# The rests of the MLP weights: added up by transfers from GpSimd's queue instead of subtracted on VectorE

## The chip, the cores and the metric

The kernel runs on one core of one Trainium2 chip. The metric is the device time of one execution in microseconds, lower is better; it is given as the median of the runs shown. The profile comes from one further execution, taken by the hardware profiler; its times are its own.

## The reference

The model is a two-layer decoder trunk for 512 tokens of width 1024, all in float32. Each layer mixes tokens by two kinds of attention, adds the result to the residual `x`, and then runs a squared-ReLU MLP. The change touches only the MLP:

```python
h = rmsnorm(x, norm_mlp)
return x + jnp.square(jax.nn.relu(h @ w_up)) @ w_down      # w_up: 1024 x 4096, w_down: 4096 x 1024
```

## The kernel before, in words

**Two-part numbers.** TensorE multiplies in a rounded 32-bit format. To keep float32's accuracy the kernel splits each operand into a rounded part `h` and a rest `lo` = operand minus `h`, and makes each product of three: `h·xh`, `h·xl` and `lo·xh` (lines 212 to 214 in `gemm`, line 1196 in `Strassen.product`). A product thus needs the rest only in its third step. The rests of weights have to be made on the chip, because the weights arrive as plain float32.

**Loaded weight tiles.** `plan` lists the weight tiles in the order of their use. `fetch` (line 164) issues the load of the next one from SyncE into a tile called `raw`, of 128x1024 numbers. `convert` (line 173) takes the oldest loaded tile, makes `wh` by a cast on ScalarE (line 186) and `wl` by a subtraction on VectorE (line 187), and then calls `fetch` for the next. `ahead`, called from inside `gemm`, converts one tile in advance. `wh` and `wl` have two buffers each.

**The MLP.** `mlp` first computes 8 of the 32 column blocks of `h @ w_up` plainly. The other 24 go through `Strassen`: twelve units, g4 to g15, each of two column blocks, made of seven products of half the size (`unit`, line 1204). Each product has 12 multiplications of 256 columns. While unit g runs, the generator `convert(g + 1)` (line 1168) makes the seven operands of the next unit: some are quarters of the loaded `w_up` tiles, some are sums of them. Two of the sums, `s1` and `s3`, are made on GpSimd (lines 1177 and 1178), the others, `s2` and `s4`, on VectorE. Each operand becomes a pair `sh` (cast on ScalarE, line 1186) and `sl` (subtraction on VectorE, line 1187). `sh` and `sl` have eight buffers each. The loads of `w_up` for unit g + 2 are issued at the start of unit g (line 1158), into two pairs of buffers that take turns.

Between the products of a unit, `unit` runs a few down products: chunks of `relu² @ w_down` over the column blocks that are done (`down`). Their weights come through `convert` of the loaded tiles; each tile serves two down products. The units have 2, 2, 3, 3, 4, 4, 4, 4, 4, 4, 2 and 0 of them. Twelve more run before the first unit. The activations that feed them get their rests on GpSimd (`act`, line 1263).

**Order and buffers.** Each engine works through its own instructions in order; a scheduler has merged the parts of the program into these orders when the kernel was built. Tiles come from pools by tag, with a fixed number of buffers (line 153), and a new user of a buffer waits for the last reader of the old one. From its seventh tile on, `w_down` is loaded into tag `crs` (line 703), which has one buffer. The Strassen sums `s` share tag `t2` with the eight residual tiles. No transfer is issued from GpSimd.

Of the kernel before, what the change touches and what calls it, by code (L numbers as in the profile page):

```python
# [11 lines left out]
F32 = mybir.dt.float32  # L12
F32R = mybir.dt.float32r
AF = mybir.ActivationFunctionType
OP = mybir.AluOpType
# [122 lines left out]
def run(*gens):  # L138
    for g in gens:
        for _ in g:  # L140
            pass


class Body:
# [28 lines left out]
    def convert(self):  # L173

        nc = self.nc
        if not self.loaded:
            self.fetch()
        if not self.loaded:
            return
        raw, src, n = self.loaded.popleft()  # L180
        if self.spots:
            h, lo = self.spots.popleft()
        else:
            h = self.t("wh", [128, 1024], F32R)
            lo = self.t("wl", [128, 1024], F32R)
        nc.scalar.copy(h[:, :n], raw[:, :n])  # L186
        nc.vector.tensor_tensor(lo[:, :n], raw[:, :n], h[:, :n].bitcast(F32), op=OP.subtract)  # L187
        self.split.append((h, lo, src, n))
        self.fetch()

# [10 lines left out]
            self.convert()  # L201

    spots = ()
    raws = deque()

    def gemm(self, ps, w, k0, xs, ks=8, start=True, stop=True):
# [705 lines left out]
    def mlp(self, l, x, u, acc, gm):  # L912

        nc, a = self.nc, self.a
        R = None
        pend = []
        acts = []

        def act(ps):
            t = self.t("tmp", [128, T])  # L920
            nc.vector.scalar_tensor_tensor(t, ps, 0.0, R, op0=OP.max, op1=OP.mult)
            h = self.t("oh", [128, T], F32R)
            lo = self.t("ol", [128, T], F32R)
            nc.scalar.activation(t, t, AF.Square)
            nc.scalar.copy(h, t)
            nc.vector.tensor_tensor(lo, t, h.bitcast(F32), op=OP.subtract)
            acts.append((h, lo))

        def down(c, m, w):

            ps = self.bank()
            yield from self.gemm(ps, w, 4 * (m % 2), acts[4 * c:4 * c + 4], ks=4)
            nc.vector.tensor_add(x[m], x[m], ps)

        def downs():
            for c in range(6):
                for m in range(8):
                    if m % 2 == 0:
                        w = self.weights(a["wd2"][l, c, m // 2])
                    yield lambda: run(down(c, m, w))  # L940

        S = Strassen(self, l, x, gm)
        D = downs()
        raws = [None] * 16
        g0 = self.PLAIN // 2
        S.load(g0)
        for j in range(self.PLAIN):
            ps = self.bank()
            w = self.weights(a["wup"][l, j].rearrange("p k c -> p (k c)"))
            run(self.gemm(ps, w, 0, u))  # L950
            if R is None and j == 0:
                pend.append(ps)
                continue
            if R is None:
                R, _ = self.rstd(acc, (self.turn_tag(), self.turn_tag()))
                prep = S.prepare(R)
                for p in pend:
                    act(p)
            act(ps)
            for _ in range(3):  # L960
                next(prep, None)
        conv = S.convert(g0)
        for i in range(12):
            next(D)()
            if i < 7:
                next(prep, None)
                next(prep, None)
            elif i == 7:
                run(prep)
            else:  # L970
                next(conv, None)
                next(conv, None)
            if i == 10:
                S.load(g0 + 1)
        run(conv)
        for g, n in zip(range(g0, 16), (2, 2, 3, 3, 4, 4, 4, 4, 4, 4, 2, 0)):
            S.load(g + 2)
            S.unit(g, D, n, acts)
        u_next = []
        acts = acts[24:]  # L980
        if l + 1 < L:
            acc = []
            self.load_small(l + 1)
            for m in range(8):
                ps = self.bank()
                w = self.weights(a["wdn"][l, m].rearrange("p k c -> p (k c)"))
                run(self.gemm(ps, w, 0, acts))
                nc.vector.tensor_add(x[m], x[m], ps)
                acc = self.sumsq(x[m], acc, m == 7)
                u_next.append(self.make_u(x[m], self.gain[:, 16 * l + 16:16 * l + 24], m))  # L990
                nc.scalar.dma_start(self.xs[m], x[m])
        else:
            self.last(x, acts, a["wdn"][l])
        self.acc = acc
        return u_next
# [105 lines left out]
class Strassen:  # L1101
# [66 lines left out]
    def convert(self, g):  # L1168

        if g == 16:  # L1170
            return
        b, nc = self.b, self.nc
        r1, r2 = self.raw.pop(g)
        a11, a12, a21, a22 = r1[:, :512], r1[:, 512:], r2[:, :512], r2[:, 512:]
        s1, s2, s3, s4 = (b.t("t2", [128, 512], name="s") for _ in range(4))
        G = nc.gpsimd
        G.tensor_tensor(s1, a21, a22, op=OP.add)
        G.tensor_tensor(s3, a11, a21, op=OP.add)
        ops = self.ops[g] = []
        for i, src in enumerate((a11, s1, s2, a22, s3, a12, s4)):  # L1180
            if i == 2:
                nc.vector.tensor_tensor(s2, s1, a11, op=OP.add)
                nc.vector.tensor_tensor(s4, s2, a12, op=OP.add)
            h = b.t("uh", [128, 512], F32R, name="sh")
            lo = b.t("ul", [128, 512], F32R, name="sl")
            nc.scalar.copy(h, src)  # L1186
            nc.vector.tensor_tensor(lo, src, h.bitcast(F32), op=OP.subtract)  # L1187
            ops.append((h, lo))
            yield

# [110 lines left out]
```

## Time and profile before

| | us |
|---|---|
| median of three runs | 1553.21 (1552.73 to 1553.71) |
| the profiled execution | 1552.95 |
| its span, first to last instruction | 1551.2 |
| TensorE busy in the span | 1536.4 (99%) |
| VectorE | 1075.2 (69%) |
| ScalarE | 776.0 (50%) |
| GpSimd | 205.2 (13%) |

PE is TensorE's multiplications, PEld its weight loads, which overlap them; DVE is VectorE, ACT ScalarE, POOL GpSimd, SPq the queue of SyncE that issues most transfers. In rows of groups the columns are the line, engine, operation, the tile written and those read with their shapes and the count; then the busy time in us and the mean of one in ns; then the engine's idle time just before these instructions and what ended it. Rows of a timeline give start and length in us.

### The profile page before, as it was taken

Reading aid. Unit: us, or ns where it says so; the run is one execution under the profiler, and the core shown is the slowest. Engines: PE = TensorE matmul, PEld = TensorE weight load, DVE = VectorE, ACT = ScalarE, POOL = GpSimd, SP = SyncE. Lnnn points to the kernel's source line nnn. Section 1 sums busy time; section 2 is a strip of 40 time slices with the busy share of each in tenths; the row PEclk is TensorE's granted clock in tenths of the full one; section 3 lists DMA queues with packets and bytes.
Section 4 is the critical chain, followed back from the end, with each engine's and each line's share of the span. In section 5 each row is a group of like instructions: output and inputs, shape, how many; then the busy total and the mean of one; then the engine's idle time right before and its main releaser. Section 6 shows DMA issues by size and latency. Waiting matters only on the chain.

```text
span 1551.2 us, 22739 instructions
## 1 busy us (share of the span) xinstructions
PE 1536.4 (99%) x8460; PEld 1306.6 (84%) x8460; DVE 1075.2 (69%) x2204; ACT 776.0 (50%) x1455; POOL 205.2 (13%) x177
## 2 busy tenths in 40 slices
PE   9999999999999999999999999999999999999997
PEld 8877888888888999999887688888888889999997
DVE  5687988766569776664646789887664887766643
ACT  6444655553454555444433456555434635545553
POOL 4000000000201232221400000000002013222222
PEclk9999999999999999999999999999999999999999
DMA  7545422133333322321535543221433333323131
GB/s 240 172 128 154 127 82 82 55 114 117 96 95 123 109 96 95 109 82 64 176 117 165 157 140 100 68 82 55 150 95 95 95 120 99 113 91 99 65 96 55
DMA packets 56638, 169.57 MB, mean 109 GB/s; under 512 B 7344, under 2 KB 8112, under 8 KB 56528
## 3 DMA queue, kind: packets, MB, share of 16 engines
q1 hardware_dynamic: 53072, 161.84, 33.5%
q10 hardware_dynamic: 3456, 6.29, 1.2%
q8 instruction: 66, 1.08, 0.3%
q14 instruction: 44, 0.36, 0.1%
HBM read 140.77 MB, written 4.19 MB: 93 GB/s over the span
## 4 chain that ended last, share of the span: by engine, by line
PE 95%; DVE 3%; ACT 1%; issue 1%; POOL 0%; DMA 0%; DVEq 0%; SPq 0%; POOLq 0%; ACTq 0%
PE ps_mm L212 12%; PE ps_mm L213 12%; PE ps_mm L214 12%; PE ps_S L1196 4%; PE ps_O L1196 4%; PE ps_O L447 4%; PE ps_mm L1196 3%; PE ps_PT L421 3%; PE ps_PT L1196 3%; PE ps_S L212 3%; PE ps_S L213 3%; PE ps_S L214 3%; PE ps_PT L212 3%; PE ps_PT L213 3%; PE ps_PT L214 3%; PE ps_O L212 3%
## 5 line engine op out<-in xcount | busy, mean ns | idle before, releaser
L186 ACT CAST wh<-raw 128x1024 fp32r<-128x1024 f32 (+2 forms) x187 | 192.6, 1030 | 263.7 <-issue 58.5
L187 DVE TENSOR_TENSOR wl<-raw,wh 128x1024 fp32r<-128x1024 f32 (+2 forms) x187 | 226.6, 1212 | 49.8 <-ACT wh L186 48.9
L212 PE MATMUL ps_mm<-uh,wh 128*128 128x512 f32 x512 | 205.1, 401 | 0.0
L214 PE MATMUL ps_mm<-uh,wl 128*128 128x512 f32 x512 | 202.3, 395 | 0.0
L213 PE MATMUL ps_mm<-ul,wh 128*128 128x512 f32 x512 | 202.1, 395 | 0.0
L399 ACT ACTIVATE E<-E,mx 128x128 f32<-128x128 f32 x192 | 108.0, 563 | 82.7 <-DVE mx L398 75.6
L430 ACT CAST pth<-ps_PT 128x512 fp32r<-128x512 f32 x144 | 73.0, 512 | 94.7 <-PE ps_PT L421 94.4
L212 PEld LDWEIGHTS ps_mm<-uh,wh 128*128 128x128 f32 x512 | 96.2, 188 | 26.5 <-issue 10.6
L214 PEld LDWEIGHTS ps_mm<-uh,wl 128*128 128x128 f32 x512 | 96.2, 188 | 20.4 <-issue 0.8
L213 PE MATMUL ps_mm<-ol,wh 128*128 128x512 f32 (+1 forms) x288 | 111.5, 387 | 1.5 <-POOL ol L1263 1.5
L212 PE MATMUL ps_mm<-oh,wh 128*128 128x512 f32 (+1 forms) x288 | 111.8, 388 | 0.0
L214 PE MATMUL ps_mm<-oh,wl 128*128 128x512 f32 (+1 forms) x288 | 111.2, 386 | 0.0
L398 DVE CUSTOM_DVE_ANT_0 E<-ps_S,ct 128x128 f32<-128x128 f32 x192 | 92.2, 483 | 26.5 <-PE ps_S L395 25.0
L213 PEld LDWEIGHTS ps_mm<-ul,wh 128*128 128x128 f32 x512 | 96.4, 188 | 15.1
L431 DVE TENSOR_TENSOR ptl<-ps_PT,pth 128x512 fp32r<-128x512 f32 x144 | 85.0, 595 | 27.6 <-ACT pth L430 27.2
L1187 DVE TENSOR_TENSOR sl<-s,sh 128x512 fp32r<-128x512 f32 x96 | 76.6, 801 | 36.6 <-ACT sh L1186 36.3
L1263 POOL TENSOR_TENSOR ol<-c,oh 128x512 fp32r<-128x512 f32 x48 | 62.7, 1306 | 295.9 <-ACT oh L1262 268.3
L1186 ACT CAST sh<-raw 128x512 fp32r<-128x512 f32 x72 | 44.7, 620 | 106.3 <-PE ps_S L1196 48.1
L1186 ACT CAST sh<-s 128x512 fp32r<-128x512 f32 x96 | 59.3, 620 | 56.4 <-PE ps_PT L1196 19.3
L253 POOL TENSOR_TENSOR acc<-sq 128x512 f32<-128x512 f32 (+1 forms) x6 | 8.4, 1394 | 595.0 <-DVE wl L187 580.1
L421 PE MATMUL ps_PT<-ct,E 128*128 128x128 f32 x480 | 82.9, 273 | 1.4 <-DVE ptl L431 1.4
L421 PEld LDWEIGHTS ps_PT<-ct,E 128*128 128x128 f32 x480 | 60.1, 140 | 14.8 <-DVE ptl L431 4.2
(441 smaller groups left out, 4068.0 us busy)
## 6 DMA issues: line engine op xcount, KB each, us to landing
raw<-wb SPq DMA_DIRECT2D x64, 512.0 KB, 3.2
raw<-wup SPq DMA_DIRECT2D x64, 512.0 KB, 3.7
raw<-wd SPq DMA_DIRECT2D x48, 512.0 KB, 3.5
kd<-hl SPq DMA_DIRECT2D x48, 256.0 KB, 4.6
w<-w SPq DMA_DIRECT2D x32, 256.0 KB, 5.8
q<-hl SPq DMA_DIRECT2D x64, 128.0 KB, 3.2
raw<-wo SPq DMA_DIRECT2D x16, 512.0 KB
raw<-wout SPq DMA_DIRECT2D x16, 512.0 KB, 3.6
```

The source lines that it names most:

```text
L186: nc.scalar.copy(h[:, :n], raw[:, :n])
L187: nc.vector.tensor_tensor(lo[:, :n], raw[:, :n], h[:, :n].bitcast(F32), op=OP.subtract)
L212: mm(ps, h[:, c], xh, start=start and i == 0, stop=False)
L213: mm(ps, h[:, c], xl, start=False, stop=False)
L214: mm(ps, lo[:, c], xh, start=False, stop=stop and i == ks - 1)
L398: nc.vector.tensor_tensor_reduce(e, ps[:, :n], self.mask[:, T - n:], -1.0, BIG, OP.add, OP.min, mx)
L399: nc.scalar.activation(e, e, AF.Exp, bias=mx, scale=-1.0, accum_out=sm[:, i:i + 1])
L421: nc.tensor.transpose(ps[:, j * 128:(j + 1) * 128], E[i][:, b * 128:(b + 1) * 128], self.ident)
L431: nc.vector.tensor_sub(lo[:, o:o + n], ps[:, :n], h[:, o:o + n].bitcast(F32))
L1186: nc.scalar.copy(h, src)
L1187: nc.vector.tensor_tensor(lo, src, h.bitcast(F32), op=OP.subtract)
L1196: self.nc.tensor.matmul(ps, w, x, skip_group_check=True, **kw)
```

## The change

`convert` and `Strassen.convert` no longer subtract on VectorE. Instead ScalarE writes the negative of the rounded part into `lo`, and a transfer issued from GpSimd adds the loaded weight (or the sum) onto it: `lo` = -`h` + operand. For the Strassen operands this holds everywhere; for loaded tiles only while the units run (`by_dma`), which covers 18 tiles of `w_down` in each layer. The casts to `h`, the buffers and the order of the calls stay as they are.

```diff
         nc.scalar.copy(h[:, :n], raw[:, :n])
-        nc.vector.tensor_tensor(lo[:, :n], raw[:, :n], h[:, :n].bitcast(F32), op=OP.subtract)
+        if self.by_dma:
+            self.rest_by_dma(h[:, :n], lo[:, :n], raw[:, :n])
+        else:
+            nc.vector.tensor_tensor(lo[:, :n], raw[:, :n], h[:, :n].bitcast(F32), op=OP.subtract)
         self.split.append((h, lo, src, n))
         self.fetch()
...
+    by_dma = False
+
+    def rest_by_dma(self, h, lo, x):
+
+        self.nc.scalar.activation(lo, h.bitcast(F32), AF.Copy, scale=-1.0)
+        self.nc.gpsimd.dma_start(lo, x, accum_op=OP.add)
...
         run(conv)
+        self.by_dma = True
         for g, n in zip(range(g0, 16), (2, 2, 3, 3, 4, 4, 4, 4, 4, 4, 2, 0)):
             S.load(g + 2)
             S.unit(g, D, n, acts)
+        self.by_dma = False
...
             nc.scalar.copy(h, src)
-            nc.vector.tensor_tensor(lo, src, h.bitcast(F32), op=OP.subtract)
+            b.rest_by_dma(h, lo, src)
             ops.append((h, lo))
```

## The prediction

> **What bounds the kernel now.** I read the page first (busy shares), then the table by stage over the two MLP stretches, then TensorE's waits, and last the chain and the timelines of one MLP unit.
>
> ```profile
> span 1551.2 us, 22739 instructions
> ...
> PE 1536.4 (99%) x8460; PEld 1306.6 (84%) x8460; DVE 1075.2 (69%) x2204; ACT 776.0 (50%) x1455; POOL 205.2 (13%) x177
> ```
>
> ```profile
> 507.00:538.00 31.00, 31.00 (x216) 28.94 (x215) 23.17 (x34) 15.61 (x27) 8.48 (x6) 1.00 0.35 107
> ```
>
> ```profile
> 507.00:726.50 219.50, 218.97 (x1432) 200.66 (x1431) 142.88 (x212) 112.17 (x185) 56.18 (x42) 1.00 0.29 97
> 575.00:701.00 126.00, 126.00 (x795) 114.35 (x795) 82.44 (x121) 64.90 (x106) 31.74 (x25) 1.00 0.28 93
> 1272.00:1480.00 208.00, 207.62 (x1338) 189.49 (x1338) 137.41 (x203) 106.27 (x174) 53.59 (x40) 1.00 0.29 94
> ```
>
> The columns after the stretch and its length are busy us of PE, PEld, DVE, ACT and POOL, then the granted clock, the DMA share and GB/s. Where the change works (units g4 to g15: 507 to 726.5 in the first layer, from 1272 in the second) TensorE stands still for 219.50 - 218.97 = 0.53 us and 208.00 - 207.62 = 0.38 us. VectorE, from which the work is taken, is busy 65% there and nobody on the path waits for it:
>
> ```profile
> PE ps_mm L213 <- POOL ol L1263: 1.5, 2, 1.1
> ...
> PE ps_PT L213 <- POOL ol L1263: 0.4, 1, 0.4
> ```
>
> These are TensorE's only waits in the MLP (us, times, longest), and both are for GpSimd. So there is nearly nothing to win: all of TensorE's idle time in both stretches is 0.9 us, 0.06% of the time. The question is only whether the new way of making the rests stays hidden.
>
> **The unit's clock.** In the chain that ended last, one unit with four down products repeats exactly:
>
> ```profile
> 1346.16 1.43 PE ps_S L1196 x12
> 1347.59 1.44 PE ps_PT L1196 x12
> ...
> 1364.92 0.23 PE ps_mm L214
> ...
> 1367.20 1.43 PE ps_S L1196 x12
> ```
>
> Start, length, instruction. The same product comes again after 1367.20 - 1346.16 = 21.04 us. Seven Strassen products of 1.44 are 10.1, so a down product is (21.04 - 10.1)/4 = 2.74 us. Units with two downs take 15.5 us and with three 18.3. A loaded tile of w_down serves two downs, so in 4-down units one tile is used up every 10.52 us.
>
> **What the change removes and adds.**
>
> ```profile
> L187 DVE TENSOR_TENSOR wl<-raw,wh 128x1024 fp32r<-128x1024 f32 x177 | 218.6, 1235 | 42.2 <-ACT wh L186 41.3 <-DMA raw<-wb 0.5 <-DMA q<-hl 0.2
> ...
> L186 ACT CAST wh<-raw 128x1024 fp32r<-128x1024 f32 x177 | 186.0, 1051 | 249.0 <-issue 58.5 <-PE ps_mm L213 51.2 <-PE ps_O L213 42.6
> ...
> L1187 DVE TENSOR_TENSOR sl<-s,sh 128x512 fp32r<-128x512 f32 x96 | 76.6, 801 | 36.6 <-ACT sh L1186 36.3
> L1263 POOL TENSOR_TENSOR ol<-c,oh 128x512 fp32r<-128x512 f32 x48 | 62.7, 1306 | 295.9 <-ACT oh L1262 268.3 <-DMA raw<-wd 9.2 <-PE ps_S L213 9.2
> ...
> L1186 ACT CAST sh<-s 128x512 fp32r<-128x512 f32 x96 | 59.3, 620 | 56.4 <-PE ps_PT L1196 19.3 <-PE ps_mm L1196 19.3 <-DVE s L1182 7.0
> ...
> L1187 DVE TENSOR_TENSOR sl<-raw,sh 128x512 fp32r<-128x512 f32 x72 | 53.2, 738 | 7.6 <-ACT sh L1186 3.4
> ```
>
> VectorE loses 96 + 72 = 168 subtractions on Strassen operands (76.6 + 53.2 = 130 us) and, by the changed program's instruction list, 36 on w_down tiles (18 a layer, 36 x 1.235 = 44 us). This relief is worth nothing, since no wait of TensorE in these stretches ends on VectorE. ScalarE gains as many negations, priced as the casts of the same shape: 168 x 0.620 + 36 x 1.051 = 142 us. Its tightest place is the two 2-down units: 15.61 busy in 31, plus 14 x 0.62 + 2 x 1.05 = 10.8, gives 26.4 of 31: hidden, if closely. GpSimd gains 204 transfers, which the trace does not show at all: nothing is issued from there before. A 4-down unit gets 7 + 2 = 9 of them. GpSimd is busy 31.74 in 126, so 5.3 in 21.04, which leaves 1.75 us for each issue. The nearest rows for an issue are GpSimd's own operations (1.306): 9 x 1.3 + 5.3 = 17 of 21.04, hidden.
>
> The seven Strassen rests have a whole unit from their cast to their use (21.04 us; 15.5 at least). Cast, negation, issue and transfer are 0.62 + 0.62 + 1.3 and a landing of some 5: hidden. What they do not pass unharmed is GpSimd's queue. In the instruction list the unit's first sum (L1177) stands behind three of the transfers and waits until the second has landed; the w_down transfer stands behind that sum, in the same queue.
>
> **The place where it is tight** is the loaded w_down tile. Its load goes to tag crs, of which there is one buffer, so the next load starts only when the last reader of the tile is done. That reader was VectorE; it becomes the transfer's landing.
>
> ```profile
> 1353.92 0.33 SPq L170 DMA_DIRECT2D raw<-wd  x1
> ...
> 1363.76 0.33 SPq L170 DMA_DIRECT2D raw<-wd  x1
> ```
>
> ```profile
> 1351.59 1.05 ACT L186 CAST wh<-raw 128x1024 fp32r<-128x1024 f32 x1 [1.97 <-PE ps_O L213]
> ...
> 1361.39 1.05 ACT L186 CAST wh<-raw 128x1024 fp32r<-128x1024 f32 x1
> ...
> 1372.63 1.05 ACT L186 CAST wh<-raw 128x1024 fp32r<-128x1024 f32 x1 [1.97 <-PE ps_O L213]
> ```
>
> ```profile
> 1352.67 1.22 DVE L187 TENSOR_TENSOR wl<-raw,wh 128x1024 fp32r<-128x1024 f32 x1 [0.17 <-ACT wh L186]
> ```
>
> ```profile
> raw<-wd SPq DMA_DIRECT2D x48, 512.0 KB, 3.5
> ```
>
> Cast at 1351.59, rest done at 1353.89, next load issued at 1353.92, landed 3.5 later at 1357.4, next cast at 1361.39. The loop has 4.0 us of slack here and 1372.63 - 1363.76 - 3.5 = 5.4 in the next turn, 4.7 in the mean. After the change the loop is cast 1.05, negation 1.05, X (from the negation's end to the transfer's landing), 0.1 for the release, load 3.5: 5.7 + X against 10.52. **It stays hidden up to X = 4.8 us.** Beyond that each tile comes later than the one before by X - 4.8. A first reserve absorbs this: from the cast at 1351.59 to the first product with the rest of that tile (1364.92) are 13.3 us.
>
> **X, from both sides.** Below: the issue at a GpSimd operation's 1.3, and a landing like that of the load of the same 512 KB, 3.5: X = 4.8. (Lower still if the issue is short: 3.5.) Above: this transfer must also read the destination it adds to, so its data time is at least that of two copies, and possibly of more.
>
> ```profile
> q1 hardware_dynamic: 53072, 161.84, 33.5%
> ```
>
> 161.84 MB took 33.5% of 16 engines' 1551.2 us, which is 3.21 us per MB on all 16, so 0.84 us for a 128x512 operand (0.262 MB) and 1.68 for a w_down tile. Twice the data adds 1.7 us, and half of a GpSimd operation standing ahead 0.65: X = 1.3 + 0.65 + 3.5 + 1.7 = 7.15. If the adding took four times a copy, X would be 10.5. I take 7.15: the second read is certain, what goes beyond is not.
>
> A rule speaks for this price: the Trainium skill, "Collectives: The Full Stack", section "The bandwidth ceiling: the fold count and why AG ≠ RS ≠ AR", says that a reduce in the DMA engines reads two sources and so runs at half the copy's rate. No transfer of the trace before shows it; by a plain copy's price X would be 5.5 with the same queueing.
>
> **Sum.** The loop is 5.7 + 7.15 = 12.85, 2.33 over 10.52. Six 4-down units use 12 tiles a layer: 12 x 2.33 = 28, less the reserve 13.3 - (1.05 + 1.05 + 7.15) = 4.0: 24. The DMA engines set a bound of their own: in 4-down units the share 0.28 is 5.9 us, and doubled copies add 2 x (7 x 0.84 + 2 x 1.68) = 18.5, 24.4 in all; this is below the loop's 2 x 12.85 = 25.7, so the loop decides. In the 3-down units it is 0.29 x 18.3 + 2 x (7 x 0.84 + 1.5 x 1.68) = 22.1, 3.8 over; in the 2-down units 0.35 x 15.5 + 2 x (7 x 0.84 + 1.68) = 20.6, 5.1 over. Two of each give 17.8, of which the Strassen operands' reserve of about a unit less its chain (15.5 - 7) absorbs 8.6: 9. A layer loses 24 + 9 = 33 us, both 66. The profiled execution took 1552.95 (span 1551.2 and 1.75 around it; 0.26 under the median 1553.21): 1552.95 + 66 = 1619, so **1620 us, 4.3% slower**.
>
> **Rivals.**
> - *Not slower (0.13).* X stays at or under 4.8. For it speaks that 1.3 + 3.5 is exactly that; against it the second read and the queue in front. It decides at X = 4.8. The time is 1552 to 1555: at best the 0.9 us of idle time go. The Trainium skill, "DMA: Bandwidth & Descriptors", section "Anatomy of one DMA", would give this one: about 2.0 us plus the bytes at 436 GB/s is an estimate of 3.2 us for the tile. No run so far shows such a transfer.
> - *GpSimd becomes the bound (0.15).* If an issue takes two GpSimd operations, 2.6 us, a 4-down unit needs 9 x 2.6 + 5.3 = 28.7, 7.7 over; a 3-down unit 8.5 x 2.6 + 5.3 = 27.4, 9.1 over; a 2-down unit 8 x 2.6 + 4.2 = 25.0, 9.5 over. 12 x 7.7 + 4 x 9.1 + 4 x 9.5 - 17 = 150: 1703 us. It starts at 1.75 us an issue. For it speaks that each carries 128 rows with three accesses; nothing in the trace prices that.
> - *The adding itself is slow (0.12).* At four copies the DMA engines need 5.9 + 37 = 42.9 in a 4-down unit, 21.9 over; with 21 over in the others 12 x 21.9 + 8 x 21 = 430: 1980 us.
>
> **How the numbers follow.** The forecast (DMA landing in the tile's loop, 1575 to 1680) has 0.60, the rivals 0.13, 0.15 and 0.12. About 0.2%, 3.1 us, is what a measurement of this kernel can tell from no change. Faster by more has 0.02: the MLP stretches hold only 0.9 us. Within 0.2% has 0.11, slower 0.87. The range reaches from the hidden case to beyond the GpSimd case, 1553 to 1780; the slow adding is left out above.
>
> **What would show it.** In the changed profile: TensorE waiting in the MLP at the third product of a down triple (the one with wl) for a transfer, about 2 us per tile after the first; loads of w_down 12.8 us apart in 4-down units in place of 9.8 and 11.2; VectorE 174 us less busy, ScalarE 142 more; a DMA share near 0.9 there against 0.28. If GpSimd's sequencer issues without pause, its rival holds. If the transfers land within 4.8 us of the negation's end, there is no loss. The prediction is wrong in size if the landing time is not near 7 us, and wrong in kind if TensorE waits on the Strassen rests (sl) first.

## The result and the profile after

The changed kernel takes **1668.84 us** (median of four runs, 1668.32 to 1669.36) against 1553.46 (four runs, 1552.73 to 1553.89) on the same chip: ratio 1.0743 (95% interval 1.0725 to 1.0762), 115 us slower. The forecast was 66 us slower. The profiled execution took 1669.36.

Line numbers in the changed kernel: the cast of a loaded tile is still L186; the negation is L211 and the transfer L212; `s1` and `s3` are L1189 and L1190, `s2` and `s4` L1194 and L1195; the Strassen cast is L1198, its product L1208. TensorE writes its products into banks of PSUM, the tiles called `ps`; L1249 is VectorE's read of the bank onto which the unit's last product is added.

The page of the kernel after: span, engines, DMA queues, and the issues with their median time to landing.

```profile
span 1667.6 us, 23307 instructions
...
PE 1566.5 (94%) x8460; PEld 1328.6 (80%) x8460; DVE 907.7 (54%) x2000; ACT 893.3 (54%) x1659; POOL 379.4 (23%) x381
...
q0 software_dynamic: 29376, 62.93, 21.0%
...
raw<-wd SPq DMA_DIRECT2D x48, 512.0 KB, 3.6
sl<-s POOLq DMA_DIRECT2D x96, 256.0 KB, 4.6
sl<-raw POOLq DMA_DIRECT2D x72, 256.0 KB, 5.3
wl<-raw POOLq DMA_DIRECT2D x36, 512.0 KB, 5.4
```

q0 is new: GpSimd's 204 transfers. The span grew by 116.4 us. TensorE's busy time grew by 1566.5 - 1536.4 = 30.1 of these, with the same 8460 multiplications, and its idle time by the other 86.3. TensorE's waits in the kernel after, longest sums first:

```profile
PE ps_S L1208 <- DVE c L1249: 44.0, 10, 12.0
PE ps_O L1208 <- DVE c L1249: 36.6, 9, 10.9
PE ps_PT L1208 <- DVE c L1249: 3.7, 1, 3.7
```

With one more of 1.0 these are 85.3 us: practically all the new idle time is a Strassen product that waits until VectorE has read its PSUM bank. No wait for `wl` or `sl` is among TensorE's large ones. VectorE is idle almost half of the time, so the next question is what it waits for itself. From the waits of all engines:

```profile
DVE s L1194 <- DMA sl<-s: 138.0, 20, 12.6
...
DVE s L1195 <- DMA sl<-s: 89.2, 17, 8.2
ACT wh L186 <- DMA raw<-wd: 80.2, 20, 8.8
```

The Strassen sums wait for the landing of transfers that still read the old sums. VectorE's timeline shows one such place:

```profile
1496.34 0.69 DVE L1194 TENSOR_TENSOR s<-s,raw 128x512 f32<-128x512 f32 x1 [5.66 <-DMA sl<-s]
...
1497.40 0.42 DVE L1249 TENSOR_TENSOR c<-y,ps_O 128x256 f32<-128x256 f32 x1
```

L1194, whose sum is cast only in the next unit, stands in VectorE's order ahead of L1249, which TensorE needs now. VectorE waits 5.66 us, then does L1194, one operation of a product (L1231) and L1249. What L1231 and L1249 read was there: TensorE had ended its last multiplication at 1495.58. Both stood behind a wait that was not their own.

The chain of waits, through one whole unit (start, length, piece), shows a loop of the unit's length:

```profile
1457.44 0.59 ACT sh L1198 x2
...
1460.08 4.88 DMA sl<-s
...
1465.08 0.47 POOL s L1190
...
1466.89 4.04 DMA sl<-s
...
1471.15 0.06 DVE s L1194
...
1472.21 0.42 DVE c L1249
...
1475.56 4.27 DMA raw<-wd
...
1479.91 1.06 ACT wh L186
...
1482.31 0.59 ACT sh L1198 x2
```

From the casts of two sums to the same casts of the next unit are 1482.31 - 1457.44 = 24.87 us, against 21.04 before. Two landings stand in it one after the other (4.88, then 4.04): the first frees the buffer for L1190, and only behind L1190 in GpSimd's order is the transfer issued whose landing frees the buffer for L1194. After L1249 the chain goes on to the load of the next w_down tile (4.27) and to its cast L186, behind which the casts of the sums stand on ScalarE. What that load had waited for is not L1249, though, but the tile's buffer: a `wl` transfer issued at 1469.02 held it until it landed, 6.5 us later. From SyncE's rows:

```profile
1462.02 0.33 SPq L170 DMA_DIRECT2D raw<-wd  x1
...
1475.56 0.33 SPq L170 DMA_DIRECT2D raw<-wd  x1
```

This is the forecast's loop: each cast waits for its load, each transfer follows its negation, each load waits for the landing of the transfer. From 1450.23 to 1552.30 nine loads lie 12.76 us apart in the mean, two to a unit. So two kinds of held buffers make two loops of about the unit's length, which meet on ScalarE, where the sums' casts stand behind the tile's.

The clock makes most of the rest. Two products of the same 12 multiplications, from the chain right after that pause, and two stretches of the table by stage (after the stretch and its length: busy PE, PEld, DVE, ACT, POOL, granted clock, DMA share, GB/s):

```profile
1497.87 2.93 PE ps_O L1208 x12
...
1503.85 1.43 PE ps_PT L1208 x12
```

```profile
1499.00:1500.00 1.00, 1.00 (x7) 1.00 (x7) 0.00 (x0) 1.00 (x3) 0.00 (x0) 0.50 1.02 205
...
1503.00:1506.00 3.00, 3.00 (x24) 2.87 (x23) 0.88 (x2) 0.62 (x1) 1.98 (x2) 1.00 0.96 218
```

After a pause of 2.3 us TensorE works at a granted clock of 0.50, and the product takes 2.93 us in place of 1.43. Summed over the table by stage in steps of 1 us, the granted clock falls in 14 such stretches of the units, and the share that is missing while TensorE is busy comes to 27.5 us: most of the 30 us of added busy time.

### The profile page after: what moved, and what is told of

The parts are those of the page before. It is cut to its first block, busy times and chain, and to the rows that moved or that the text cites. A ratio compares the mean times of both kernels' runs of the same rounds, so it can differ in the third digit from the quotient of the medians.

```text
span 1667.6 us, 23307 instructions
## 1 busy us (share of the span) xinstructions
PE 1566.5 (94%) x8460; PEld 1328.6 (80%) x8460; DVE 907.7 (54%) x2000; ACT 893.3 (54%) x1659; POOL 379.4 (23%) x381
## 3 DMA queue, kind: packets, MB, share of 16 engines
q0 software_dynamic: 29376, 62.93, 21.0%
## 4 chain that ended last, share of the span: by engine, by line
PE 72%; DMA 13%; issue 5%; ACT 4%; DVE 3%; POOL 3%; SPq 0%; DVEq 0%; POOLq 0%; ACTq 0%
PE ps_mm L222 10%; PE ps_mm L223 10%; PE ps_mm L224 10%; DMA sl<-s 8%; PE ps_O L457 4%; PE ps_PT L431 3%; PE ps_PT L222 2%; PE ps_S L1208 2%; PE ps_PT L223 2%; PE ps_PT L224 2%; PE ps_S L222 2%; PE ps_S L223 2%; PE ps_S L224 2%; PE ps_S L402 2%; PE ps_O L222 2%
## 5 line engine op out<-in xcount | busy, mean ns | idle before, releaser
L186 ACT CAST wh<-raw 128x1024 fp32r<-128x1024 f32 (+2 forms) x187 | 192.4, 1029 | 298.9 <-DMA raw<-wd 80.2
L190 DVE TENSOR_TENSOR wl<-raw,wh 128x1024 fp32r<-128x1024 f32 (+2 forms) x151 | 180.3, 1194 | 43.5 <-ACT wh L186 42.7
L212 POOL DMA_DIRECT2D sl<-s x96 | 89.4, 994 | 148.3 <-ACT sl L211 127.6
L211 ACT ACTIVATE sl<-sh 128x512 fp32r<-128x512 f32 x168 | 102.8, 626 | 2.4
L1194 DVE TENSOR_TENSOR s<-s,raw 128x512 f32<-128x512 f32 x24 | 18.7, 780 | 147.8 <-DMA sl<-s 138.0
L212 POOL DMA_DIRECT2D sl<-raw x72 | 67.8, 942 | 136.6 <-PE ps_S L223 46.1
L1195 DVE TENSOR_TENSOR s<-s,raw 128x512 f32<-128x512 f32 x24 | 19.2, 799 | 103.8 <-DMA sl<-s 89.2
```

Source lines behind the costliest of these rows:

```text
L211: self.nc.scalar.activation(lo, h.bitcast(F32), AF.Copy, scale=-1.0)
L212: self.nc.gpsimd.dma_start(lo, x, accum_op=OP.add)
```

## The experiments

The theories. **A** (in later texts also **C**): the transfers hold the sums' buffers until they land; the engine that has to refill them waits, and what stands behind it in its order waits too. **B**: the forecast's loop, the single buffer of the loaded w_down tile. **D**: what decides is how much the transfers load the DMA engines. **E**: whichever engine refills the sums carries the delay, so that moving them only moves it. Every edit is to the changed kernel, and "loss" is the median less that of the kernel before on the same chip (1554.16 in the first four, 1553.46 in the next four, 1553.62 in the last).

**Sums in buffers of their own.**

```diff
-        s1, s2, s3, s4 = (b.t("t2", [128, 512], name="s") for _ in range(4))
+        s1, s2, s3, s4 = (b.t(t, [128, 512], name="s") for t in ("t2", "r", "t2", "small"))
```

> The change, but the sums s2 and s4, which VectorE makes, each get a buffer of their own (two tiles that lie idle in the MLP), so that the four buffers of t2 serve s1 and s3 alone. Theory A: the transfers hold the sums' buffers until they land, VectorE waits in order for such a buffer (227 us in all at L1194 and L1195 of the changed kernel), and TensorE behind it for PSUM: 1560 to 1600 us, and VectorE's wait for a transfer of sl falls under 40 us. Theory B (the one buffer of the loaded w_down tile decides, as forecast): 1655 us or more, the waits of ScalarE for raw<-wd stay at 80 us.

Measured: 1715.05 us, ratio 1.1035 (1.1018 to 1.1051), 161 us lost: slower than the change itself. Two views, VectorE's and ScalarE's waits and TensorE's:

```profile
DVE s L1195 <- DMA sl<-s: 200.6, 19, 14.9
ACT wh L186 <- DMA raw<-wd: 186.9, 28, 13.5
```

```profile
PE ps_S L1208 <- DVE c L1249: 22.6, 9, 5.5
PE ps_PT L224 <- DMA wl<-raw: 22.5, 9, 4.0
PE ps_mm L224 <- DMA wl<-raw: 22.5, 9, 5.1
```

`s1` and `s3` have two buffers each now, but `s2` and `s4` one each, so VectorE still waits; and TensorE now waits for `wl` as well (45 us). The edit did not take the wait away that it aimed at, so it doesn't refute A; it shows the tile's loop (B) next to it.

**The w_down rests added from the weights in HBM**, so that the transfer no longer reads the loaded tile and its buffer comes free at the cast.

```diff
-            self.rest_by_dma(h[:, :n], lo[:, :n], raw[:, :n])
+            self.rest_by_dma(h[:, :n], lo[:, :n], src)
```

> The change, but the transfer that makes the rest of a w_down tile reads the weights from HBM again and not from the loaded tile, so that the tile's one buffer is free after the cast. Theory A: 1640 us or more, ScalarE's wait for raw<-wd (80 us) goes without much effect. Theory B: 1555 to 1590 us.

Measured: 1689.67 us, ratio 1.0871 (1.0854 to 1.0887), 136 us lost: slower again, though the wait aimed at is nearly gone. From the waits of this kernel:

```profile
DVE s L1194 <- DMA sl<-s: 151.5, 20, 14.1
...
ACT wh L186 <- DMA raw<-wd: 18.1, 3, 8.7
```

ScalarE's wait for w_down fell from 80.2 to 18.1 us, and TensorE gained nothing: its waits for L1249 are longer than before (49.6 us for ps_S alone, against 44.0). So freeing the tile's buffer wins nothing here: the sums' waits remain. Why the time is even longer isn't shown; the `wl` transfers land later (7.5 us from the issue in place of 5.4), now that w_down comes twice from HBM.

**Both edits.**

> Both edits: own buffers for s2 and s4, and the w_down rests from HBM. Theories A and B together: 1553 to 1565 us. If it stays above 1580, a third cause is at work (the transfers' landing time, GpSimd's queue or ScalarE's added work).

Measured: 1659.81 us, ratio 1.0685 (1.0667 to 1.0703), 106 us lost. Each edit alone made it slower, both together a little faster than the change. Waits of VectorE for the sums remain (185.0 and 97.8 us), because the single buffers of `s2` and `s4` are still held.

**The w_down rests back on VectorE; the Strassen rests stay with the transfers.**

```diff
-        self.by_dma = True
+        self.by_dma = False
```

> One part alone: the Strassen rests by transfers, the w_down rests by VectorE as before. Theory A: 1630 to 1670 us. Theory B: 1553 to 1560 us.

Measured: 1647.72 us, ratio 1.0608 (1.0588 to 1.0627), 94 us lost. The 168 Strassen transfers alone bring 94 of the 115 us. A 4-down unit (from ScalarE's copy L1236 in one unit to that in the next, mean of both layers) takes 24.6 us here, against 21.1 before and 25.7 with the whole change.

**Only the operands that are plain quarters of w_up, only the sums, only w_down.** All three leave the rest of the work to VectorE; the first two set `by_dma` to `False` in the units as well.

```diff
-            b.rest_by_dma(h, lo, src)
+            if i in (0, 3, 5):
+                b.rest_by_dma(h, lo, src)
+            else:
+                nc.vector.tensor_tensor(lo, src, h.bitcast(F32), op=OP.subtract)
```

> Only the three Strassen rests whose source is a quarter of a loaded tile by transfer (72 transfers); the rests of the sums and of the w_down tiles by VectorE as before. No transfer holds a sum. Theory C (VectorE's own two sums stand in its queue before the readers of PSUM and wait for buffers that transfers hold): 1553 to 1562 us, no wait of VectorE for a transfer. Theory D (the transfers' landing or their load on the DMA engines delays TensorE by itself): in proportion to 72 of 168 transfers, about 1590 us.

The second has `i not in (0, 3, 5)` in its place:

> The other part: only the four rests of the sums by transfer (96 transfers), all others by VectorE. Theory C: nearly the whole loss of the run with only the Strassen rests, 1615 to 1650 us. Theory D: in proportion to 96 of 168, about 1605 us, with VectorE's waits for transfers below 60 us.

The third subtracts in the Strassen operands always and keeps `by_dma`:

```diff
-            b.rest_by_dma(h, lo, src)
+            nc.vector.tensor_tensor(lo, src, h.bitcast(F32), op=OP.subtract)
```

> Only the 36 rests of the w_down tiles by transfer, the Strassen rests by VectorE. This is the forecast's loop alone: with X at 7.15 us as forecast 1590 to 1610 us; if the transfer lands within 4.8 us of the negation's end, 1553 to 1558 us.

Measured: the quarters 1555.61 us, ratio 1.0014 (1.0005 to 1.0024), 2 us lost; the sums 1581.09, ratio 1.0173 (1.0157 to 1.0188), 28 us; w_down 1567.18, ratio 1.0083 (1.0066 to 1.0100), 14 us. VectorE's waits in the second, then ScalarE's and TensorE's in the third; in the first none of VectorE's larger waits is for a transfer:

```profile
DVE s L1194 <- DMA sl<-s: 9.7, 2, 5.1
```

```profile
ACT wh L186 <- DMA raw<-wd: 111.7, 26, 7.3
```

```profile
PE ps_mm L224 <- DMA wl<-raw: 0.5, 1, 0.5
```

72 transfers that hold no sum cost next to nothing; 96 that hold them cost 28. A proportion by count, as D has it, would give the first 72/96 of the second, 21 us. With w_down alone the loop of the forecast runs: ScalarE waits for the loads, yet a 4-down unit takes only 22.2 us.

The two Strassen parts do not add up: 2 + 28 = 30, but both together 94. With those of w_down they nearly do: 94 + 14 = 108, and 115 in all. Part of the reason for the first stands in VectorE's order. First the kernel with all Strassen transfers, then the one with the sums alone (three lines longer, so L1249 is L1252):

```profile
1452.82 0.69 DVE L1194 TENSOR_TENSOR s<-s,raw 128x512 f32<-128x512 f32 x1 [5.68 <-DMA sl<-s]
1453.42 0.41 DVE L1249 TENSOR_TENSOR c<-y,ps_O 128x256 f32<-128x256 f32 x1
```

```profile
621.94 0.41 DVE L1252 TENSOR_TENSOR c<-y,ps_S 128x256 f32<-128x256 f32 x1
...
623.51 0.69 DVE L1194 TENSOR_TENSOR s<-s,raw 128x512 f32<-128x512 f32 x1 [0.83 <-issue]
```

In the kernel before, in the changed one and in the one with all Strassen transfers, every unit's `s2` stands ahead of the PSUM read. In the one with the sums alone the scheduler put it behind the read in all but two of the units that make one. There `s2` waits for transfers only twice (9.7 us, against 87.0 with all Strassen transfers), and mostly TensorE's bank has been read by then. That kernel thus differs by its order too, which is why its 28 us are not a clean price of the sums' transfers, and less than theory A had asked.

**Copies in place of additions.** The transfer overwrites the negated part with the operand, so the addition is missing; the buffers and the waits are those of the change.

```diff
-        self.nc.gpsimd.dma_start(lo, x, accum_op=OP.add)
+        self.nc.gpsimd.dma_start(lo, x)
```

> The changed kernel with plain copies in place of the adding transfers: the rest becomes the operand itself, so the addition is left out. Same issues, same waits, half the reads. If the adding costs as much as a second copy: the landing of sl falls from 4.6 to 5.3 us to 3.5 to 4, the software queue's share of the DMA engines halves from 21.0%, and the time falls to 1600 to 1640 us. If the landing is set by fixed costs: within 15 us of 1669.

Measured: 1592.72 us, ratio 1.0250 (1.0234 to 1.0265), 39 us lost in place of 115. From its page:

```profile
q0 software_dynamic: 29376, 62.93, 12.2%
...
sl<-s POOLq DMA_DIRECT2D x96, 256.0 KB, 3.2
...
wl<-raw POOLq DMA_DIRECT2D x36, 512.0 KB, 3.3
```

The order of `s2` ahead of the read is the change's, and VectorE still waits for the sums (76.2 and 59.3 us), but for landings of 3.2 in place of 4.6 us. That agrees with a loss sized by how long a buffer is held, but doesn't single it out: the copies also halve GpSimd's issue (0.53 in place of 0.99 us) and nearly halve the queue's share of the DMA engines.

**`s2` and `s4` on GpSimd**, so that VectorE has no wait for a sum's buffer; and the same with w_down's rests from HBM.

```diff
-                nc.vector.tensor_tensor(s2, s1, a11, op=OP.add)
-                nc.vector.tensor_tensor(s4, s2, a12, op=OP.add)
+                G.tensor_tensor(s2, s1, a11, op=OP.add)
+                G.tensor_tensor(s4, s2, a12, op=OP.add)
```

> The full change, but all four sums are made on GpSimd, so that nothing VectorE does in the units waits for a transfer. Theory C (VectorE's wait for sum buffers, ahead of its reads of PSUM, is the main loss): 1570 to 1610 us, TensorE's waits for VectorE (85 us) below 20 us. Theory E (any engine that must refill the sums' buffers carries the delay on; the transfers' landing around the ring of four buffers sets the pace): 1640 us or more, with the waits moved to GpSimd and to the casts behind it.

> All four sums on GpSimd and the w_down rests added from HBM. Theory C with B: 1553 to 1575 us. Theory E: 1630 us or more.

Measured: 1719.88 us, ratio 1.1078 (1.1060 to 1.1097), 166 us lost; from HBM 1712.71, ratio 1.1023 (1.1006 to 1.1039), 159 us. TensorE's and GpSimd's waits in the first of them:

```profile
PE ps_PT L224 <- DMA wl<-raw: 37.3, 9, 9.5
PE ps_mm L224 <- DMA wl<-raw: 33.6, 8, 7.7
```

```profile
POOL s L1195 <- DMA sl<-s: 93.4, 19, 6.6
...
POOL s L1194 <- DMA sl<-s: 68.4, 20, 5.3
...
POOL s L1189 <- DMA sl<-s: 49.7, 20, 3.4
```

VectorE's queue is free, TensorE's longest wait for L1249 is 4.4 us, and the time is worse. GpSimd waits for the buffers 211.5 us, and GpSimd is the engine that issues the transfers: `wl` comes late, and TensorE waits for that. This is E. That VectorE's queue is the one place of the damage is refuted by it.

**Two buffers for each sum.** `s3` is written over the loaded quarter `a21`, and `s4` takes two tags in turn; then also with w_down's rests from HBM.

```diff
-        s1, s2, s3, s4 = (b.t("t2", [128, 512], name="s") for _ in range(4))
+        s1, s2, s4 = (b.t(t, [128, 512], name="s") for t in ("t2", "t2", ("r", "small")[g % 2]))
+        s3 = a21
```

> The full change, with two buffers for every sum: s1 and s2 share the four of t2, s4 alternates between two tiles that lie idle in the MLP, and s3 is written over the quarter a21 that nobody needs after it. A sum is then overwritten only when its transfer of two units before has landed. Theories C and E: 1567 to 1600 us (what is left is the loop of the w_down tile, 14 us alone); VectorE's wait for transfers of sl below 30 us. Theory D (the transfers' load on the DMA engines and their landing by themselves): 1640 us or more.

> The same two buffers for every sum, and the w_down rests added from HBM, so that the w_down tile is free after its cast. Theories C and E with the forecast's loop B: 1553 to 1565 us. Theory D: within 15 us of the run with two buffers alone.

Measured: 1722.78 us, ratio 1.1093 (1.1077 to 1.1110), 169 us lost; from HBM 1659.99, ratio 1.0702 (1.0656 to 1.0747), 106 us. The waits of the first (its lines are one higher):

```profile
DVE s L1195 <- POOL s L1190: 229.8, 20, 20.0
ACT wh L186 <- DMA raw<-wd: 206.3, 28, 14.5
...
POOL s L1190 <- DMA raw<-wup: 93.9, 20, 9.6
```

No sum waits for a sum's transfer any more, but the loaded quarter is now held by one: the load of the next `w_up` comes late, `s1` with it, and VectorE's `s2` waits for `s1`. The test was not clean, since it moved the held buffer to the loaded tiles. Sums with two buffers that hold nothing else were not tried.

## Why the prediction was right in direction and short in size

- **TensorE bounds; nothing to win.** Right: the best of the parts, the quarters alone, takes VectorE's work away and comes out 0.14% (0.05 to 0.24) slower.
- **The engines' shares.** VectorE lost 1075.2 - 907.7 = 167.5 us (forecast 174), ScalarE gained 893.3 - 776.0 = 117.3 (forecast 142). The sum of single negations is near the forecast; on the page adjacent ones overlap.
- **GpSimd's issue.** The groups of GpSimd after, and in the kernel with copies:

```profile
L212 POOL DMA_DIRECT2D sl<-s x96 | 89.4, 994 | 148.3 <-ACT sl L211 127.6 <-issue 18.3 <-POOL ol L1275 1.5
```

```profile
L212 POOL DMA_DIRECT2D sl<-s x96 | 51.1, 533 | 143.2 <-ACT sl L211 108.3 <-issue 24.1 <-DVE x L943 8.3
```

  Columns behind the bar: busy us, mean ns of one, idle time before. An issue takes 0.99 us (0.91 for `wl`), under the 1.3 assumed and far under the 2.6 of the rival, which is false: GpSimd is busy 23%.
- **What adding costs.** Right in kind. The queue's 21.0% of 1667.6 us are 350 us for 62.93 MB, 5.57 us per MB; as copies 12.2% of 1590.8, 194 us, 3.08 per MB. Adding costs 1.8 copies where 2 were taken, so the rival of four is false. The rule of the Trainium skill that was weighed ("Collectives: The Full Stack", "The bandwidth ceiling: the fold count and why AG ≠ RS ≠ AR": a reduce reads two sources, at half the rate) is borne out nearly (1.8); the plain price by "DMA: Bandwidth & Descriptors", "Anatomy of one DMA", an estimate of 3.2 us for the tile, holds for the copy (3.3) and not for the addition (5.4).
- **The DMA engines' share.** Forecast near 0.9; the table by stage over the units of the first layer has 0.85 (next to last column):

```profile
508.00:781.60 273.60, 230.03 (x1407) 208.17 (x1406) 65.65 (x118) 166.26 (x278) 137.78 (x138) 0.93 0.85 182
```

- **The tile's loop.** Right as a mechanism, smaller than said. X was set at 7.15. With w_down alone a 4-down unit takes 22.2 us, 11.1 per tile, which by the forecast's own 5.7 + X is X = 5.4, near the 5.1 us from issue to landing in that kernel. Twelve tiles a layer at 11.1 - 10.52 are 7.0, both layers 14, and 13.7 were measured. The wait at the third down product, which was to show it, is 0.5 us there.
- **The step that failed** is "the seven Strassen rests ... hidden". Their chain was compared with the use of `sl` a unit later, and to `sl` it is indeed hidden. But the transfer also reads the sum, and holds its buffer until it lands. The refill of that buffer is an instruction on VectorE, in the same order as before the change, ahead of the PSUM read for which TensorE waits. Alone the Strassen rests cost 94 us, where the sum had 9 us a layer, and these for the load on the DMA engines in the 2- and 3-down units. The prediction had noted the same thing on GpSimd (the unit's first sum behind the landing of the second transfer) and didn't ask for `s2` and `s4`. TensorE's waiting place was to be `wl`, or else `sl`; it is L1249 (85 us).
- **The sum.** 4-down units take 25.7 us in the mean, as forecast. The forecast's loop does run in them, with its sign: loads 12.76 us apart, where 12.8 was said. That the size fits is luck in two terms: X is about 6.0 (12.76 less cast, negation, release and load) in place of 7.15, and the load takes 4.6 in place of 3.5. Nor does this loop alone make the units long: without it they take 24.6. They cost 12 x (25.7 - 21.1) = 55 us. The 2- and 3-down units lost 25.6 and 24.4 us in the two layers where 9 each was forecast: the reserve of 8.6 was one for `sl`, and the held sums have none. The rest, some 10 us, lies before and after these units. The clock, some 27 us of the whole, is in no term of the forecast.

**What stays open.** Held sums and the held w_down tile make two loops of nearly the same length, and the runs show that taking either kind of transfer away brings much (101 us without the Strassen transfers, 21 without those of w_down), that freeing the tile's buffer alone brings nothing, and that copies in place of additions bring 76. What each is worth inside the whole isn't settled, since every edit that freed a buffer held another or moved an order. Load on the DMA engines isn't excluded as a part: in the 4-down units the tile's load takes 4.6 us from its issue to the cast with the Strassen transfers beside it and 3.7 without, and the loss rises with the queue's engine time over the parts (2 us at 106, 28 at 142, 39 at 194, 94 at 250, 115 at 350), but not alone: w_down alone loses 14 at 110, and the single buffers with and without HBM (357 and 360 us) lose 106 and 161. A 4-down unit's transfers need 2.88 MB x 5.57 + 5.9 = 22 us of its 25.7. No version beat the kernel before. An order with `s2` behind the PSUM read and all transfers kept was not tried.

## What to carry to other kernels

A transfer that takes over an engine's operation holds its source until it lands: ask not only when the result is needed but who refills the source, and what stands behind that refill in the same engine's order. Parts that cost little alone (2 and 28 us) can cost much together (94); measure them alone and together. Taking work from an engine on which nobody waits wins nothing, however busy it is.

## What the runs showed of the hardware

- **A pause can cost twice.** After 2.3 us without multiplications the granted clock was 0.50 from 1497.87 to about 1501.3, 3.4 us of work. After another pause, of 3.71 us, the first 1.4 us went on at full clock and the fall came then (granted clock 1.00, 0.78 and 0.50 in the three microseconds from 602, of which the first and the last are shown):

```profile
602.00:603.00 1.00, 0.83 (x7) 0.83 (x8) 1.00 (x3) 0.52 (x1) 0.00 (x0) 1.00 1.03 281
...
604.00:605.00 1.00, 1.00 (x6) 1.00 (x6) 0.42 (x1) 0.97 (x3) 0.90 (x2) 0.50 0.77 315
```

  After a third pause, of 3.04 us (until 1550.84), the clock stayed at 1.00, so not every pause is followed by a fall.

  The Trainium skill, "TensorE: Matmul & The Clock Gate", "Part 1: The HAM clock gate (the "warmup" mystery)", has a free-running window of about 3.4 us, whose place against the work isn't fixed. The late fall and the length of the slow stretch agree; that an idle stretch of a whole window is needed does not: 2.3 us were enough here.
- **An addition by transfer** costs about 1.8 times a copy in the DMA engines (5.57 against 3.08 us per MB) and in GpSimd's issue (0.99 against 0.53 us).
